# Engine order, edge layout and block exit changed together in a small message-passing kernel

## The chip, the cores and the metric

One core of a Trainium2 chip. The metric is the device time of one execution in microseconds. The kernel before takes 10.4 us, so this is a program of some 110 small instructions in which latencies and waits decide, not throughput.

The profile's span (first to last instruction) is shorter than the device time, 8.6 of 10.4 us before, and the difference stays out of the profile.

## The reference

128 nodes with 64 features, 512 edges with 32 features. Each edge makes a message from its source node and its own features, and each destination node takes the mean of its messages:

```python
src, dst = edge_index[0], edge_index[1]
for i in range(len(src)):
    msg_input = np.concatenate([node_features[src[i]], edge_features[i]])
    msg = np.maximum(0, msg_input @ W_msg)
    messages[dst[i]] += msg
    counts[dst[i]] += 1
return node_features + messages / np.maximum(counts, 1)[:, None]
```

## The kernel before

Gather and scatter are matmuls with one-hot matrices. The 512 source indices are cast to bf16, broadcast over 128 partitions by a matmul with ones, and compared with the partition number: this gives `gt_bf` (node x edge; its two halves are gt A and gt B below). `nf^T gt` (the gather) puts the source nodes' features, transposed, into the upper 64 rows of `xt_bf`; the edge features, transposed by TensorE, go into the lower 32. `xt_bf^T W` is the messages, a relu makes `m_bf`. A second one-hot, `d_bf` (edge x destination), sums messages and counts. Edges come in four chunks of 128; half A is chunks 0 and 1 (VectorE), half B chunks 2 and 3 (ScalarE).

The parts that the change touches, cut:

```python
# ScalarE
act.dma_start(ef_sb, edge_features.rearrange("(c p) f -> p c f", p=128))
act.dma_start(dcol_sb, bass.AP(ei_handle, n_edges, [[1, 128], [128, n_chunks]]))
wait(act, s_ef);   act.copy(ef_bf, ef_sb)
wait(act, s_xnTB); act.copy(xt_bf[0:node_dim, nhalf:n_edges], xnTB_ps)
wait(act, s_mB);   act.activation(m_bf[:, 2:4, :], mB_ps, Relu)
# VectorE, after the two casts of the source indices and the two halves of gt_bf
wait(dve, s_tp);   dve.tensor_copy(xt_bf[node_dim:feat_dim, :], efT_ps)   # transposed features
wait(dve, s_xnTA); dve.tensor_copy(xt_bf[0:node_dim, 0:nhalf], xnTA_ps)   # half A
wait(dve, s_dcf);  dve.tensor_tensor(d_bf[:, 0:2, :], ..., is_equal)      # one-hot A
dve.tensor_tensor(d_bf[:, 2:4, :], ..., is_equal)                         # one-hot B
wait(dve, s_mA);   dve.tensor_scalar(m_bf[:, 0:2, :], mA_ps, 0.0, max)    # relu A
...                                     # maximum of counts, reciprocal, result
# all engines
block = E(nc.Block(no_gpsimd_drain=True))
```

## Time and profile before

The median of 15 runs is 10.40 us (10.39 to 10.41). How to read the views: a timeline line is start, length (us), engine, source line, operation, output and inputs, shapes, and in brackets how long the engine sat idle and what ended that. The chain is followed back from the last instruction.

| Point in the profile before | us |
|---|---|
| source cast starts (index DMA has landed) | 2.26 |
| features' cast, start to end | 3.03 to 3.33 |
| transposes start | 3.38 |
| relu B ends (ScalarE) / relu A ends (VectorE) | 5.65 / 5.75 |
| result (last VectorE instruction) starts | 6.36 |
| span / device time | 8.6 / 10.40 |

The lines behind it are in the prediction below. "Front" means the part up to the transposes.

### The profile page before, as it was taken

Reading aid. Unit: us, or ns where it says so; the run is one execution under the profiler, and the core shown is the slowest. Engines: PE = TensorE matmul, PEld = TensorE weight load, DVE = VectorE, ACT = ScalarE, POOL = GpSimd, SP = SyncE. Lnnn points to the kernel's source line nnn. Section 1 sums busy time; section 2 is a strip of 40 time slices with the busy share of each in tenths; the row PEclk is TensorE's granted clock in tenths of the full one; section 3 lists DMA queues with packets and bytes.
Section 4 is the critical chain, followed back from the end, with each engine's and each line's share of the span. In section 5 each row is a group of like instructions: output and inputs, shape, how many; then the busy total and the mean of one; then the engine's idle time right before and its main releaser. Section 6 shows DMA issues by size and latency. Waiting matters only on the chain.

```text
span 8.6 us, 112 instructions
## 1 busy us (share of the span) xinstructions
PE 2.8 (32%) x20; PEld 1.4 (16%) x20; DVE 4.4 (51%) x17; ACT 2.2 (26%) x4; POOL 1.1 (13%) x9
## 2 busy tenths in 40 slices
PE   0000000000009983999991097099800000000000
PEld 0000000000004403928000090089000000000000
DVE  0001658910597099994989999975858000000000
ACT  0000000099999994000006900920000000000000
POOL 0801930000000090195000000000000000000000
DMA  0000000029969300000000000000000000060000
GB/s 0 0 0 0 0 0 0 19 43 146 197 77 62 60 7 0 0 0 0 0 0 0 0 0 0 0 0 0 0 0 0 0 0 0 1 148 4 0 0 0
DMA packets 1458, 0.16 MB, mean 19 GB/s; under 512 B 1457, under 2 KB 1457, under 8 KB 1458
## 3 DMA queue, kind: packets, MB, share of 16 engines
q10 hardware_dynamic: 1056, 0.07, 8.2%
q1 hardware_dynamic: 402, 0.09, 5.1%
HBM read 0.13 MB, written 0.03 MB: 19 GB/s over the span
## 4 chain that ended last, share of the span: by engine, by line
DVE 24%; ACT 18%; ACTq 11%; PE 10%; issue 5%; DVEq 0%
ACT L179 15%; PE efT_ps L220 7%; ACTq L171 6%; DVE xt_bf L346 5%; ACTq L162 5%; DVE xt_bf L344 5%; DVE d_bf L358 4%; DVE d_bf L349 4%; ACT ef_bf L179 4%; DVE res_sb L383 3%; PE cnt_ps L269 3%; DVE rcnt_sb L380 2%; DVE cnt_sb L378 2%; DVEq L42 0%
## 5 line engine op out<-in xcount | busy, mean ns | idle before, releaser
L179 ACT ACT_TABLE_LOAD x1 | 1.3, 1283 | 1.7 <-PEq L412 1.7
L198 PE MATMUL bankA_ps<-src_bf,ones_bf 1*128 1x256 bf16 x1 | 0.4, 388 | 2.6 <-DVE src_bf L316 2.6
L182 ACT CAST xt_bf<-bankB_ps 64x256 bf16<-64x256 f32 x1 | 0.4, 366 | 1.3 <-PE bankB_ps L236 1.3
L220 PE MATMUL efT_ps<-ident_bf,ef_bf 128*32 128x128 bf16 x4 | 0.6, 307 | 0.2 <-ACT ef_bf L179 0.2
L331 DVE TENSOR_SCALAR gt_bf<-bankA_ps,pidx_f 128x256 bf16<-128x256 f32 x1 | 0.5, 483 | 0.3 <-PE bankA_ps L198 0.3
L301 DVE MEMSET ones_bf<- 1x128 bf16 x1 | 0.2, 165 | 0.8 <-PEq L412 0.8
L316 DVE CAST src_bf<-ei_row 1x256 bf16<-1x256 int32 x1 | 0.3, 282 | 0.5 <-DMA ei_row<-in_edge_index_dram 0.5
L198 PEld LDWEIGHTS bankA_ps<-src_bf,ones_bf 1*128 1x128 bf16 x1 | 0.1, 98 | 2.6 <-DVE src_bf L316 2.6
L133 POOL CAST nf_bf<-nf_sb 128x64 bf16<-128x64 f32 x1 | 0.2, 236 | 1.9 <-DMA nf_sb<-in_node_features_dram 1.9
L344 DVE COPY xt_bf<-efT_ps 32x512 bf16<-32x512 bf16 x1 | 0.4, 415 | 0.1
L338 DVE TENSOR_SCALAR gt_bf<-bankB_ps,pidx_f 128x256 bf16<-128x256 f32 x1 | 0.5, 475 | 0.0
L346 DVE CAST xt_bf<-bankA_ps 64x256 bf16<-64x256 f32 x1 | 0.4, 417 | 0.0
L229 PE MATMUL bankA_ps<-gt_bf,nf_bf 128*64 128x256 bf16 x1 | 0.4, 423 | 0.0
L236 PE MATMUL bankB_ps<-gt_bf,nf_bf 128*64 128x256 bf16 x1 | 0.4, 421 | 0.0
L220 PEld LDWEIGHTS efT_ps<-ident_bf,ef_bf 128*32 128x32 bf16 x4 | 0.3, 127 | 0.5 <-ACT ef_bf L179 0.5
L247 PE MATMUL mA_ps<-w_bf,xt_bf 96*128 96x64 bf16 x2 | 0.3, 238 | 0.4 <-DVE xt_bf L346 0.4
L358 DVE TENSOR_TENSOR d_bf<-iota_bf,dcol_f 128x256 bf16<-128x256 bf16 x1 | 0.4, 410 | 0.0
L349 DVE TENSOR_TENSOR d_bf<-iota_bf,dcol_f 128x256 bf16<-128x256 bf16 x1 | 0.4, 409 | 0.0
L209 PE MATMUL bankB_ps<-src_bf,ones_bf 1*128 1x256 bf16 x1 | 0.4, 402 | 0.0
L186 ACT ACTIVATE m_bf<-mB_ps 128x128 bf16<-128x128 f32 x1 | 0.3, 277 | 0.4 <-PE mB_ps L258 0.4
L269 PE MATMUL cnt_ps<-onescol_bf,d_bf 128*128 128x1 bf16 x4 | 0.3, 170 | 0.3 <-DVE d_bf L358 0.3
L383 DVE SCALAR_TENSOR_TENSOR res_sb<-agg_ps,rcnt_sb,nf_sb 128x64 f32<-128x64 f32 x1 | 0.3, 283 | 0.1
(28 smaller groups left out, 5.1 us busy)
## 6 DMA issues: line engine op xcount, KB each, us to landing
ef_sb<-in_edge_features_dram ACTq DMA_DIRECT2D x1, 64.0 KB, 2.0
nf_sb<-in_node_features_dram SPq DMA_DIRECT2D x1, 32.0 KB, 1.8
out_dram<-res_sb SPq DMA_DIRECT2D x1, 32.0 KB, 1.5
w_sb<-in_W_msg_dram SPq DMA_DIRECT2D x1, 24.0 KB, 1.9
ei_row<-in_edge_index_dram SPq DMA_DIRECT2D x1, 4.0 KB
dcol_sb<-in_edge_index_dram ACTq DMA_DIRECT2D x1, 4.0 KB, 2.4
```

The source lines that it names most:

```text
L171: act.dma_start(dcol_sb[:, :], bass.AP(ei_handle, n_edges, [[1, 128], [128, n_chunks]]),),
L179: done(act.copy(ef_bf[:, :, :], ef_sb[:, :, :]), s_efbf)
L198: pe.matmul(bcastA_ps, ones_bf[:, :], src_bf[:, 0:nhalf], start=True, stop=True,),
L220: mm = pe.transpose(efT_ps[:, c * ncol : (c + 1) * ncol], ef_bf[:, c, :], ident_bf[:, :],)
L269: mm = pe.matmul(cnt_ps[:, :], d_bf[:, c, :], onescol_bf[:, :], start=(c == 0), stop=(c == n_chunks - 1),)
L331: dve.tensor_scalar(gt_bf[:, 0:nhalf], bcastA_ps, pidx_f[:, 0:1], None, ALU.is_equal),
L338: dve.tensor_scalar(gt_bf[:, nhalf:n_edges], bcastB_ps, pidx_f[:, 0:1], None, ALU.is_equal),
L344: done(dve.tensor_copy(xt_bf[node_dim:feat_dim, :], efT_ps[:, :]), s_xtef)
L346: done(dve.tensor_copy(xt_bf[0:node_dim, 0:nhalf], xnTA_ps), s_xcA)
L349: dve.tensor_tensor(d_bf[:, 0:2, :], bass.AP(iota_bf, 0, [[128, 128], [0, 2], [1, 128]]), bass.AP(dcol_f, 0, [[n_chunks, 128], [1, 2], [0, ...
L358: dve.tensor_tensor(d_bf[:, 2:4, :], bass.AP(iota_bf, 0, [[128, 128], [0, 2], [1, 128]]), bass.AP(dcol_f, 2, [[n_chunks, 128], [1, 2], [0, ...
L383: dve.scalar_tensor_tensor(res_sb[:, :], agg_ps[:, :], rcnt_sb[:, 0:1], nf_sb[:, :], ALU.mult, ALU.add,),
```

## The change

The intent: fewer and larger pieces per DMA, a shorter front on ScalarE, and less queueing on VectorE. Its core, cut (renamings `nhalf` to `wa` and `2` to `n_a`, and PSUM tensors that become separate, are left out):

```diff
-            edge_features.rearrange("(c p) f -> p c f", p=128)      # ScalarE: 512 pieces of 128 B
+            edge_features.rearrange("(p c) f -> p c f", c=n_chunks) # 128 pieces of 512 B
-            act.dma_start(dcol_sb, AP(ei_handle, n_edges, [[1, 128], [128, n_chunks]]))
+            sync.dma_start(dcol_sb, AP(ei_handle, n_edges, [[n_chunks, 128], [1, n_chunks]]))
+            wait(act, s_tp)
+            act.copy(xt_bf[node_dim:feat_dim, :], efT_ps)           # from VectorE
-            two casts src_bf[:, 0:nhalf], src_bf[:, nhalf:n_edges]
+            one cast src_bf[:, :]
-                    src_bf[:, 0:nhalf],                             # broadcast matmul, read dense
+                    bass.AP(src_bf, 0, [[n_edges, 1], [1, n_a], [n_chunks, ncol]]),
 VectorE:
-            transposed features; half A; one-hot A; one-hot B; relu A
+            one-hot A; half A; one-hot B; relu A
 TensorE:
-            wait(pe, s_dB); four count matmuls
+            wait(pe, s_dA); two count matmuls; wait(pe, s_dB); two count matmuls
-        block = E(nc.Block(no_gpsimd_drain=True))
+        block = E(nc.Block())
```

More of the change, by code (lines that the diff above doesn't have):

```diff
@@ L27, in bass_mpnn_update_kernel @@
     ncol = n_edges // n_chunks
-    nhalf = n_edges // 2
+    n_a = 2
+    wa = n_a * ncol
+    wb = n_edges - wa
     ei_handle = edge_index.tensor
@@ L68, in bass_mpnn_update_kernel @@
         rcnt_sb = E(nc.sbuf_tensor("rcnt_sb", [128, 1], fp32))
+        act_dummy = E(nc.sbuf_tensor("act_dummy", [128, 1], fp32))
         res_sb = E(nc.sbuf_tensor("res_sb", [n_nodes, node_dim], fp32))
-        bankA_ps = E(nc.psum_tensor("bankA_ps", [128, n_edges], fp32))
-        bankB_ps = E(nc.psum_tensor("bankB_ps", [128, n_edges], fp32))
+        bcastA_t = E(nc.psum_tensor("bcastA_ps", [128, wa], fp32))
+        xnTA_t = E(nc.psum_tensor("xnTA_ps", [node_dim, wa], fp32))
+        bankB_ps = E(nc.psum_tensor("bankB_ps", [128, 2 * wb], fp32))
         efT_ps = E(nc.psum_tensor("efT_ps", [edge_dim, n_edges], bf16))
-        mA_ps = E(nc.psum_tensor("mA_ps", [128, 2 * node_dim], fp32))
-        mB_ps = E(nc.psum_tensor("mB_ps", [128, 2 * node_dim], fp32))
+        mA_ps = E(nc.psum_tensor("mA_ps", [128, n_a * node_dim], fp32))
+        mB_ps = E(nc.psum_tensor("mB_ps", [128, (n_chunks - n_a) * node_dim], fp32))
         cnt_ps = E(nc.psum_tensor("cnt_ps", [n_nodes, 1], fp32))
         agg_ps = E(nc.psum_tensor("agg_ps", [n_nodes, node_dim], fp32))
-        bcastA_ps = bankA_ps[:, 0:nhalf]
-        bcastB_ps = bankB_ps[:, 0:nhalf]
-        xnTA_ps = bankA_ps[0:node_dim, nhalf:n_edges]
-        xnTB_ps = bankB_ps[0:node_dim, nhalf:n_edges]
+        bcastA_ps = bcastA_t[:, :]
+        xnTA_ps = xnTA_t[:, :]
+        bcastB_ps = bankB_ps[:, 0:wb]
+        xnTB_ps = bankB_ps[0:node_dim, wb : 2 * wb]
         s_ei = _Sig("s_ei", 16)
@@ L92, in bass_mpnn_update_kernel @@
         s_efbf = _Sig("s_efbf")
-        s_sqA = _Sig("s_sqA")
-        s_sqB = _Sig("s_sqB")
+        s_sq = _Sig("s_sq")
         s_bcA = _Sig("s_bcA")
@@ L156, in _ @@
             done(sync.dma_start(nf_sb[:, :], node_features), s_nf, 16)
+            done(
+                sync.dma_start(
+                    dcol_sb[:, :],
+                    bass.AP(ei_handle, n_edges, [[n_chunks, 128], [1, n_chunks]]),
+                ),
+                s_dc,
+                16,
+            )
             done(sync.dma_start(w_sb[:, :], W_msg), s_w, 16)
@@ L163, in _ @@
                     ef_sb[:, :, :],
-                    edge_features.rearrange("(c p) f -> p c f", p=128),
+                    edge_features.rearrange("(p c) f -> p c f", c=n_chunks),
                 ),
@@ L168, in _ @@
             )
-            with nc.allow_non_contiguous_dma(reason="dst column gather"):
-                done(
-                    act.dma_start(
-                        dcol_sb[:, :],
-                        bass.AP(ei_handle, n_edges, [[1, 128], [128, n_chunks]]),
-                    ),
-                    s_dc,
-                    16,
-                )
             wait(act, s_ef)
             done(act.copy(ef_bf[:, :, :], ef_sb[:, :, :]), s_efbf)
+            wait(act, s_tp)
+            done(act.copy(xt_bf[node_dim:feat_dim, :], efT_ps[:, :]), s_xtef)
             wait(act, s_xnTB)
-            done(
-                act.copy(xt_bf[0:node_dim, nhalf:n_edges], xnTB_ps), s_xcB
-            )
+            done(act.copy(xt_bf[0:node_dim, wa:n_edges], xnTB_ps), s_xcB)
             wait(act, s_mB)
@@ L186, in _ @@
                 act.activation(
-                    m_bf[:, 2:4, :],
-                    mB_ps[:, :].rearrange("p (c d) -> p c d", c=2),
+                    m_bf[:, n_a:n_chunks, :],
+                    mB_ps[:, :].rearrange("p (c d) -> p c d", c=n_chunks - n_a),
                     ACTF.Relu,
@@ L195, in _ @@
         def _(pe):
-            wait(pe, s_sqA, s_cst)
+            wait(pe, s_sq, s_cst)
             done(
@@ L206, in _ @@
             )
-            wait(pe, s_sqB)
             done(
@@ L211, in _ @@
                     ones_bf[:, :],
-                    src_bf[:, nhalf:n_edges],
+                    bass.AP(src_bf, n_a, [[n_edges, 1], [1, n_chunks - n_a], [n_chunks, ncol]]),
                     start=True,
@@ L228, in _ @@
             done(
-                pe.matmul(
-                    xnTA_ps, nf_bf[:, :], gt_bf[:, 0:nhalf], start=True, stop=True
-                ),
+                pe.matmul(xnTA_ps, nf_bf[:, :], gt_bf[:, 0:wa], start=True, stop=True),
                 s_xnTA,
@@ L236, in _ @@
                 pe.matmul(
-                    xnTB_ps,
-                    nf_bf[:, :],
-                    gt_bf[:, nhalf:n_edges],
-                    start=True,
-                    stop=True,
+                    xnTB_ps, nf_bf[:, :], gt_bf[:, wa:n_edges], start=True, stop=True
                 ),
@@ L245, in _ @@
             wait(pe, s_xcA, s_xtef, s_wbf)
-            for c in range(2):
+            for c in range(n_a):
                 mm = pe.matmul(
@@ L253, in _ @@
                 )
-                if c == 1:
+                if c == n_a - 1:
                     done(mm, s_mA)
             wait(pe, s_xcB)
-            for c in range(2, 4):
+            for c in range(n_a, n_chunks):
                 mm = pe.matmul(
-                    mB_ps[:, (c - 2) * node_dim : (c - 1) * node_dim],
+                    mB_ps[:, (c - n_a) * node_dim : (c - n_a + 1) * node_dim],
                     xt_bf[:, c * ncol : (c + 1) * ncol],
@@ L264, in _ @@
                 )
-                if c == 3:
+                if c == n_chunks - 1:
                     done(mm, s_mB)
+            wait(pe, s_dA)
+            for c in range(n_a):
+                pe.matmul(
+                    cnt_ps[:, :],
+                    d_bf[:, c, :],
+                    onescol_bf[:, :],
+                    start=(c == 0),
+                    stop=False,
+                )
             wait(pe, s_dB)
-            for c in range(n_chunks):
+            for c in range(n_a, n_chunks):
                 mm = pe.matmul(
@@ L272, in _ @@
                     onescol_bf[:, :],
-                    start=(c == 0),
+                    start=False,
                     stop=(c == n_chunks - 1),
@@ L277, in _ @@
                     done(mm, s_cntps)
-            wait(pe, s_reluA, s_dA)
-            for c in range(2):
+            wait(pe, s_reluA)
+            for c in range(n_a):
                 pe.matmul(
@@ L287, in _ @@
             wait(pe, s_reluB)
-            for c in range(2, 4):
+            for c in range(n_a, n_chunks):
                 mm = pe.matmul(
@@ L293, in _ @@
                     start=False,
-                    stop=(c == 3),
+                    stop=(c == n_chunks - 1),
                 )
-                if c == 3:
+                if c == n_chunks - 1:
                     done(mm, s_agg)
@@ L316, in _ @@
                 dve.tensor_copy(
-                    src_bf[:, 0:nhalf],
-                    bass.AP(eir32.tensor, 0, [[2 * n_edges, 1], [2, nhalf]]),
-                ),
-                s_sqA,
-            )
-            done(
-                dve.tensor_copy(
-                    src_bf[:, nhalf:n_edges],
-                    bass.AP(eir32.tensor, 2 * nhalf, [[2 * n_edges, 1], [2, nhalf]]),
-                ),
-                s_sqB,
+                    src_bf[:, :],
+                    bass.AP(eir32.tensor, 0, [[2 * n_edges, 1], [2, n_edges]]),
+                ),
+                s_sq,
             )
@@ L331, in _ @@
                 dve.tensor_scalar(
-                    gt_bf[:, 0:nhalf], bcastA_ps, pidx_f[:, 0:1], None, ALU.is_equal
+                    gt_bf[:, 0:wa], bcastA_ps, pidx_f[:, 0:1], None, ALU.is_equal
                 ),
@@ L338, in _ @@
                 dve.tensor_scalar(
-                    gt_bf[:, nhalf:n_edges], bcastB_ps, pidx_f[:, 0:1], None, ALU.is_equal
+                    gt_bf[:, wa:n_edges], bcastB_ps, pidx_f[:, 0:1], None, ALU.is_equal
                 ),
@@ L342, in _ @@
             )
-            wait(dve, s_tp)
-            done(dve.tensor_copy(xt_bf[node_dim:feat_dim, :], efT_ps[:, :]), s_xtef)
-            wait(dve, s_xnTA)
-            done(dve.tensor_copy(xt_bf[0:node_dim, 0:nhalf], xnTA_ps), s_xcA)
             wait(dve, s_dcf, s_ibf)
@@ L349, in _ @@
                 dve.tensor_tensor(
-                    d_bf[:, 0:2, :],
-                    bass.AP(iota_bf, 0, [[128, 128], [0, 2], [1, 128]]),
-                    bass.AP(dcol_f, 0, [[n_chunks, 128], [1, 2], [0, 128]]),
+                    d_bf[:, 0:n_a, :],
+                    bass.AP(iota_bf, 0, [[128, 128], [0, n_a], [1, 128]]),
+                    bass.AP(dcol_f, 0, [[n_chunks, 128], [1, n_a], [0, 128]]),
                     ALU.is_equal,
@@ L356, in _ @@
             )
+            wait(dve, s_xnTA)
+            done(dve.tensor_copy(xt_bf[0:node_dim, 0:wa], xnTA_ps), s_xcA)
             done(
                 dve.tensor_tensor(
-                    d_bf[:, 2:4, :],
-                    bass.AP(iota_bf, 0, [[128, 128], [0, 2], [1, 128]]),
-                    bass.AP(dcol_f, 2, [[n_chunks, 128], [1, 2], [0, 128]]),
+                    d_bf[:, n_a:n_chunks, :],
+                    bass.AP(iota_bf, 0, [[128, 128], [0, n_chunks - n_a], [1, 128]]),
+                    bass.AP(dcol_f, n_a, [[n_chunks, 128], [1, n_chunks - n_a], [0, 128]]),
                     ALU.is_equal,
@@ L368, in _ @@
                 dve.tensor_scalar(
-                    m_bf[:, 0:2, :],
-                    mA_ps[:, :].rearrange("p (c d) -> p c d", c=2),
+                    m_bf[:, 0:n_a, :],
+                    mA_ps[:, :].rearrange("p (c d) -> p c d", c=n_a),
                     0.0,
```

## The prediction

> **What bounds the kernel now.** I read four views: the page's rows by line, the DMA issues, the chain that ended last, and the timeline. The chain comes first, because a 10.4 us program of 112 small instructions is a matter of latencies, not of busy shares (no engine is above 51% of the span). Columns: start us, length us, what.
>
> ```profile
> 0.74 0.40 ACTq L162
> ...
> 1.17 0.53 ACTq L171
> ...
> 1.73 1.28 ACT L179
> ...
> 3.03 0.31 ACT ef_bf L179
> ...
> 3.38 0.62 PE efT_ps L220 x4
> ...
> 4.02 0.39 DVE xt_bf L344
> ...
> 4.47 0.42 DVE xt_bf L346
> 4.88 0.33 DVE d_bf L349
> 5.22 0.34 DVE d_bf L358
> ...
> 5.61 0.28 PE cnt_ps L269 x4
> ```
>
> The end is set by the edge features. ScalarE issues two DMAs, loads its table, casts the features; TensorE transposes them; VectorE copies the transpose out, then works through a queue of its own (node half A, two builds of the one-hot d_bf); after the last build come the counts, their reciprocal and the result at 6.36 us. There is a second chain beside it, from the source indices. It is on no page of the critical chain, but the timeline has it (start us, length us, engine, line, tile):
>
> ```profile
> 2.26 0.28 DVE L316 CAST src_bf<-ei_row 1x256 bf16<-1x256 int32 x1 [0.50 <-DMA ei_row<-in_edge_index_dram]
> 2.60 0.39 PE L198 MATMUL bankA_ps<-src_bf,ones_bf 1*128 1x256 bf16 x1 [2.60 <-DVE src_bf L316]
> 3.02 0.48 DVE L331 TENSOR_SCALAR gt_bf<-bankA_ps,pidx_f 128x256 bf16<-128x256 f32 x1 [0.28 <-PE bankA_ps L198]
> 3.42 0.47 DVE L338 TENSOR_SCALAR gt_bf<-bankB_ps,pidx_f 128x256 bf16<-128x256 f32 x1
> 4.13 0.42 PE L236 MATMUL bankB_ps<-gt_bf,nf_bf 128*64 128x256 bf16 x1
> 4.58 0.37 ACT L182 CAST xt_bf<-bankB_ps 64x256 bf16<-64x256 f32 x1 [1.26 <-PE bankB_ps L236]
> 5.37 0.28 ACT L186 ACTIVATE m_bf<-mB_ps 128x128 bf16<-128x128 f32 x1 [0.42 <-PE mB_ps L258]
> 5.47 0.28 DVE L368 TENSOR_SCALAR m_bf<-mA_ps 128x128 bf16<-128x128 f32 x1
> 5.81 0.29 PE L280 MATMUL agg_ps<-m_bf,d_bf 128*128 128x64 bf16 x2
> ```
>
> Half B of the messages is ready at 5.37 + 0.28 = 5.65 us on ScalarE. The aggregation does not start until 5.81, because half A's relu on VectorE, though its matmul (first start 4.94) was long done, sat behind the two d_bf builds and ended at 5.75; the counts are later still. So VectorE's queue between 4.0 and 5.75 us is the bound of the tail, and the front of the chain (ScalarE's DMA issues and table load) delays when that queue begins.
>
> **What the Trainium skill says.** (1) "ScalarE: Activation LUTs", section What ACT_TABLE_LOAD costs: about 1283 ns for a load. The trace has 1283 ns, and it begins at 1.73 us, right behind the second DMA issue (1.17 + 0.53 = 1.70) and not behind the features. (2) Same page and section: an ACTIVATE with immediate scale and bias takes 186 ns + 0.833 N ns. For N = 256 that is 399 ns; the trace has 366 (L182), for N = 128 from PSUM 277 (L186) against 293. It is a few per cent high here. (3) "SBUF — State Buffer", the note on 16-byte cachelines in the port section: at least two hits per line are needed for full bandwidth. No strided bf16 read by TensorE is in this trace, so it cannot agree or disagree. (4) "DMA: Bandwidth & Descriptors", the summary table: 512 B or more per descriptor for line rate. The page of before has 1457 of 1458 packets under 512 B; the two ScalarE DMAs, whose patterns make 512 pieces each, took 2.0 and 2.4 us to landing, the 32 KB node features 1.8.
>
> **The change part by part.**
>
> *The DMA layout.* Edge p·4+c instead of c·128+p: the features become 128 pieces of 512 B instead of 512 of 128 B, the destinations 128 pieces of 32 B instead of 512 of 8 B. The destination DMA moves to SyncE between node features and weights. ScalarE loses 0.53 us of issue, so its table load starts at about 1.17 to 1.20 and ends near 2.48. The features I take to land at 2.5 (estimate: 0.74 + 1.8, the node features' landing, for 2.0). The cast is then 2.5 to 2.85 instead of 3.03 to 3.33. That is up to 0.5 us off the front of the old chain. On SyncE the third issue at 1.51 is now the destinations; with 1.8 to 1.9 to landing they arrive at about 3.4 (3.57 before), cast by GpSimd by 3.6. The weights slip by one issue, 0.4 us, from 1.51 to 1.9; landing 1.9 later is 3.8, cast done by about 4.1; needed at 4.75. Neither binds.
>
> *One source cast instead of two.* A 128x1 cast takes 155 ns (L304), a 1x256 one 282 ns: 127 ns for 255 elements, 0.5 ns each (128x128 at 218 ns gives the same slope). So 1x512 takes 155 + 511 x 0.5 = 410 ns. It replaces a first half that was ready after 282, so the start of the index chain is 0.13 us later. This is a loss.
>
> *The transpose copy moves from VectorE to ScalarE.* Off VectorE: 0.415 us (L344) and its wait for the transposes. On ScalarE: by the slope of 277 to 366 ns per 128 elements, 366 + 2 x 89 = 544 ns; by the skill's formula 613. Transposes now run about 3.1 to 3.7, so the copy ends at 4.3 to 4.35, before ScalarE's next work (4.5). Hidden.
>
> *Order on VectorE.* The first d_bf build goes into the hole before node half A, the second after it; the relu of half A then meets no queue. Counts are split, so two of four matmuls run early.
>
> *The index chain, which should now set the end*, with lengths and gaps from the rows above. Source cast 2.26 + 0.41 = 2.67; gap 0.06 (2.54 to 2.60), broadcast A 2.73; 0.42 from matmul to VectorE, gt A 3.15, ending 3.63; 0.40 from start to start, gt B 3.55, ending 4.02; gap 0.05, gather matmul B 4.07; 0.45 to ScalarE, copy B 4.52 to 4.89; gap 0.05, message matmuls B 4.94; 0.33 (5.04 to 5.37), relu B 5.27 to 5.55; gap 0.06, aggregation B 5.61; 0.30 for both matmuls and 0.05 to VectorE, result 5.96.
>
> *VectorE beside it.* d_bf A 3.95 (0.40 after gt B), half A copy 4.28 (0.33 later) to 4.70, d_bf B 4.62 to 5.03. Message matmuls A 4.75, relu A 4.75 + 0.33 = 5.08 to 5.36. Counts 5.08; 0.30 to their maximum 5.38; 0.20 to the reciprocal 5.58; 0.25 to the result 5.83. That is 0.13 earlier than 5.96, so aggregation B decides.
>
> The result then starts at 5.96 instead of 6.36: minus 0.40 us. The output DMA and the end are unchanged. The 1.8 us between the 8.6 us span and the 10.4 us time I take as constant. 10.40 - 0.40 = 10.00; I add 0.02 for the block's exit (below).
>
> *PSUM split, unused act_dummy.* No instruction, no time. In before, no reader of bankA overlaps a writer (gt A ends 3.50, its next matmul starts 3.91).
>
> *The default block exit.* It drops the option that leaves out a GpSimd drain. No page that I found gives its length, and before has none. GpSimd's last cast ends at 3.98 (about 4.1 after the change) and the output lands at 6.67 + 1.5 = 8.17, so 4 us of drain would be hidden if it runs before the engines meet.
>
> **The rivals.** (a) *The drain costs at the end.* If it, or a heavier barrier, stands after the output's landing, its length adds in full: from 0.2 us (gain down to 0.2, time 10.2) to more than 0.4 (no gain). For: before spends 0.4 us after landing on the exit, so what the exit does is visible. Against: GpSimd is idle for half of the kernel. (b) *The strided read of src_bf is slow.* Two bf16 values 8 B apart share a 16-byte line, just the two hits that the skill asks. If it failed and the matmul streamed at half speed, 0.1 to 0.2 us would come on the index chain: 10.1 to 10.2. (c) *The index DMA lands earlier.* It is one 4 KB packet and shares engines with the features' 512 packets; with 128 of them it may land sooner and everything follows: 9.8 to 9.9. Against: the DMA row shows 19 GB/s in the slice from 1.5 to 1.72 us, which is 4 KB, just its size, before the bulk. (d) *The moved load waits.* If the destinations landed after 3.8 us, the first d_bf build, now ahead of half A in VectorE's order, would hold that half: 0.1 to 0.3 us worse.
>
> **Range and chances.** Centre 10.02. (c) or a shorter cast gives 9.8; (a) or (b) at moderate size 10.3. Faster by 2% means below 10.19: it takes the loss of more than 0.17 of 0.38 to miss. I give 0.74 to that, 0.20 to within 2%, and 0.06 to slower, which nearly only a costly exit could bring.
>
> **What would show it.** Right: table load at about 1.2; features' cast ending before 2.9; a source cast of about 410 ns; gt A near 3.15; no VectorE queue ahead of relu A; result near 5.96; the chain running from the index DMA over half B and the relu on ScalarE. Wrong: broadcast to gt A over 0.5 us (b); d_bf A waiting for the destinations (d); a span longer by more than the result's shift (a); a result that starts on time and a time that does not follow (the exit outside the span).

## The result, and the profile after

The median of 11 runs is 9.88 us (9.82 to 10.02), against 10.40 for before in the same session. The ratio is 0.948 (95% interval 0.9455 to 0.9504). Ratios here are the mean time of one kernel's fast runs over that of the other's of the same rounds, so they are not quite the ratio of the quoted medians. A run is labelled slow here when it is over 1.5% above the fastest run of its kernel; three of these eleven are (10.00 to 10.02).

The chain of the kernel after (start us, length us, what):

```profile
0.74 1.40 DMA ei_row<-in_edge_index_dram
...
2.16 0.43 DVE src_bf L320
...
2.64 0.41 PE bcastA_ps L200
...
3.47 0.47 DVE gt_bf L335
3.94 0.33 DVE d_bf L342
4.27 0.34 DVE xt_bf L351
...
4.66 0.30 PE mA_ps L242 x2
...
4.98 0.30 DVE m_bf L363
...
5.33 0.29 PE agg_ps L284 x2
5.62 0.22 PE agg_ps L293 x2
...
5.86 0.28 DVE res_sb L378
```

It begins with another DMA: not the features but the source indices. The table load, 15% of the chain before, is gone from it. After gt B it runs over half A on VectorE. That half will turn out not to be the one that decides. What lies beside it, from the timeline of after:

```profile
1.13 1.28 ACT L181 ACT_TABLE_LOAD   x1 [1.13 <-PEq L407]
...
2.53 0.30 ACT L181 CAST ef_bf<-ef_sb 128x128 bf16<-128x128 f32 x1
...
3.18 0.61 PE L221 MATMUL efT_ps<-ident_bf,ef_bf 128*32 128x128 bf16 x4
...
3.82 0.57 ACT L183 COPY xt_bf<-efT_ps 32x512 bf16<-32x512 bf16 x1 [0.99 <-PE efT_ps L221]
...
3.90 0.47 POOL L147 CAST w_bf<-w_sb 96x64 bf16<-96x64 f32 x1 [0.50 <-DMA w_sb<-in_W_msg_dram]
...
4.00 0.42 PE L235 MATMUL bankB_ps<-gt_bf,nf_bf 128*64 128x256 bf16 x1
...
5.20 0.28 ACT L188 ACTIVATE m_bf<-mB_ps 128x128 bf16<-128x128 f32 x1 [0.38 <-PE mB_ps L253]
...
5.53 0.29 PE L293 MATMUL agg_ps<-m_bf,d_bf 128*128 128x64 bf16 x2
```

The features are ready at 2.83 us, 0.50 earlier than before, but the transposes start at 3.18, only 0.20 earlier: TensorE takes its work in program order, and the broadcast matmuls, now the later ones (2.64 and 2.85), stand ahead. In eight more profiles whose features were ready earlier the transposes follow the second broadcast by the same 0.33 or 0.34 us. Relu B ends at 5.48 and half B's aggregation starts at 5.53, right behind it.

A table of three intervals sorts the difference of the two profiled runs, and serves for every experiment:

| Profiled run | A: source cast starts | B: cast to result | C: result to end of device time | Time |
|---|---|---|---|---|
| before | 2.26 | 4.10 | 4.04 | 10.40 |
| after | 2.16 | 3.70 | 3.97 | 9.83 |
| difference | -0.10 | -0.40 | -0.07 | -0.57 |

B is the work between the landing of the indices and the result. C is the profiled run's time minus the start of the result, so it holds the result, the output's DMA, the exit and what lies outside the span. The table sorts the difference; it doesn't yet say what caused it, since in before the front, and not the landing of the indices, sets when the result starts.

### The profile page after: what moved, and what is told of

It reads as the page before. It is cut to its first block, busy times and chain, and to the rows that moved or that the text cites. A ratio compares the mean times of both kernels' runs of the same rounds, so it can differ in the third digit from the quotient of the medians.

```text
span 8.0 us, 107 instructions
## 1 busy us (share of the span) xinstructions
PE 2.9 (36%) x20; PEld 1.4 (18%) x20; DVE 3.9 (49%) x15; ACT 2.8 (35%) x5; POOL 1.4 (18%) x9
## 4 chain that ended last, share of the span: by engine, by line
DVE 30%; DMA 17%; PE 15%; issue 6%
DMA ei_row<-in_edge_index_dram 17%; DVE gt_bf L335 6%; DVE src_bf L320 5%; PE bcastA_ps L200 5%; DVE xt_bf L351 4%; DVE d_bf L342 4%; PE mA_ps L242 4%; DVE m_bf L363 4%; PE agg_ps L284 4%; DVE res_sb L378 4%; DVE gt_bf L328 3%; PE agg_ps L293 3%
## 5 line engine op out<-in xcount | busy, mean ns | idle before, releaser
L183 ACT COPY xt_bf<-efT_ps 32x512 bf16<-32x512 bf16 x1 | 0.6, 572 | 1.0 <-PE efT_ps L221 1.0
L328 DVE TENSOR_SCALAR gt_bf<-bcastA_ps,pidx_f 128x256 bf16<-128x256 f32 x1 | 0.5, 484 | 0.5 <-PE bcastA_ps L200 0.5
L147 POOL CAST w_bf<-w_sb 96x64 bf16<-96x64 f32 x1 | 0.5, 465 | 0.5 <-DMA w_sb<-in_W_msg_dram 0.5
```

Of the source, the lines that this page charges most:

```text
L147: done(pool.tensor_copy(w_bf[:, :], w_sb[:, :]), s_wbf)
L183: done(act.copy(xt_bf[node_dim:feat_dim, :], efT_ps[:, :]), s_xtef)
L328: dve.tensor_scalar(gt_bf[:, 0:wa], bcastA_ps, pidx_f[:, 0:1], None, ALU.is_equal),
```

## The experiments

The theory to test: the engine order gives the 0.40 us of B; the layout's gain at the front lies off the path; the new end is set by the index chain through half B. The rivals: the layout, or the exit, is what pays; half A sets the end, as the profile's chain has it.

Each experiment is after with the edit shown, if not said otherwise.

### One part at a time: exit, layout, order

**after_no_drain** and **before_drain** swap the exits of the two kernels.

```diff
 after_no_drain:
-        block = E(nc.Block())
+        block = E(nc.Block(no_gpsimd_drain=True))
 before_drain (from before):
-        block = E(nc.Block(no_gpsimd_drain=True))
+        block = E(nc.Block())
```

> The kernel after with the block exit of before (GpSimd drain left out again). My account: the exit's drain is hidden behind 4 us of idle GpSimd, so the time stays at 9.88 us within 0.05, ratio 0.945 to 0.953. Rival (a), the default exit costs something after the output's landing: the time falls by what it costs, to 9.7 or less, and the tail from the result to the end of the span shrinks.

> The kernel before with the default block exit of after, the same question from the other side, on a kernel whose runs scatter by only 0.02 us. My account: 10.40 within 0.03. Rival (a): 10.5 or more.

Before with the default exit takes 10.34 us (10.31 to 10.36) against 10.40, ratio 0.9935 (0.9919 to 0.9951). The profiles have the result at 6.36 us in both, so nothing moved ahead of it; C falls from 4.04 to 3.96, and the page counts 109 instructions instead of 112. After without it: 10.02 us (9.91 to 10.19), three of six runs with the slow label; the fast ones give 0.9533 (0.9519 to 0.9548) instead of 0.948, and C is 4.05. In all twelve profiles with the default exit C is 3.95 to 3.99, in the two without it 4.04 and 4.05. The drain is not merely hidden, as I had it; the exit that has it is shorter by 0.06 to 0.08 us on both kernels. That is the opposite of my allowance and of rival (a). Which of its instructions saves the time, the profile doesn't show.

The profiled run of after_no_drain was one of its slow ones, at 10.12 us:

```profile
2.37 0.41 DVE L320 CAST src_bf<-ei_row 1x512 bf16<-1x512 int32 x1 [0.61 <-DMA ei_row<-in_edge_index_dram]
...
6.07 0.28 DVE L378 SCALAR_TENSOR_TENSOR res_sb<-agg_ps,rcnt_sb,nf_sb 128x64 f32<-128x64 f32 x1 [0.22 <-PE agg_ps L293]
```

B is again 3.70 us (6.07 - 2.37). All of the delay lies in A: the indices landed 1.61 us after their issue instead of 1.40. The clock is the same. So what is labelled slow here is the late landing of one DMA. The other profiled run with that label (two_casts, cast at 2.35) shows it too, and so do two of runs labelled fast (features_later and delay_a).

**layout_only** keeps the layout, the queues, the merged cast and the exit, and gives VectorE and ScalarE back their old order; the counts wait for both one-hots.

```diff
 ScalarE:
-            wait(act, s_tp)
-            act.copy(xt_bf[node_dim:feat_dim, :], efT_ps)
 VectorE:
-            one-hot A; half A; one-hot B
+            wait(dve, s_tp)
+            dve.tensor_copy(xt_bf[node_dim:feat_dim, :], efT_ps)
+            half A; one-hot A; one-hot B
```

> The change's data layout alone: features and destinations contiguous per partition, destinations on SyncE's queue, one source cast, but VectorE's old order (transpose copy on VectorE, half A, then both one-hot builds). My account, stepped through with the durations of after: one-hot B ends 5.40, counts 5.45, result 6.20 instead of 6.36, so about 10.2 us (0.16 off). Rival, the layout is the main part because it takes 0.5 us off the old front: 9.95 or less.

10.51 us (10.33 to 10.58), ratio of fast runs 0.9974 (0.9936 to 1.0013): no gain. Four of the six runs carry the slow label. The profiled run is the fastest, 10.33 us:

```profile
3.95 0.42 DVE L339 COPY xt_bf<-efT_ps 32x512 bf16<-32x512 bf16 x1
...
5.63 0.19 PE L262 MATMUL cnt_ps<-onescol_bf,d_bf 128*128 128x1 bf16 x2 [0.36 <-DVE d_bf L353]
...
6.36 0.28 DVE L378 SCALAR_TENSOR_TENSOR res_sb<-agg_ps,rcnt_sb,nf_sb 128x64 f32<-128x64 f32 x1
```

Its result starts at 6.36, just where it does in before, and the 0.07 us are the exit's (C is 3.97). My 6.20 was too early in two places: half A follows the 512-column copy on VectorE by 0.45 us, as it does in before, where I had 0.38; and this variant's counts start at 5.63, 0.15 after one-hot B instead of 0.06. The second isn't the layout's doing but, it seems, the variant's, in which TensorE waits there for both one-hots; so the layout with the old order may be worth up to 0.09 us. The rival, that the layout is the main part, falls all the same. The features' cast ends 0.42 us earlier than in before (2.91), but VectorE's old queue starts only 0.07 earlier (3.95 for 4.02): it now stands behind gt B, so behind the index chain. The PSUM split is in this run too; with the old order it brings no gain either.

**order_only** keeps the order and the exit, and takes layout, queues and the two source casts from before.

```diff
-            edge_features.rearrange("(p c) f -> p c f", c=n_chunks)
+            edge_features.rearrange("(c p) f -> p c f", p=128)
-            sync.dma_start(dcol_sb, AP(ei_handle, n_edges, [[n_chunks, 128], [1, n_chunks]]))
+            act.dma_start(dcol_sb, AP(ei_handle, n_edges, [[1, 128], [128, n_chunks]]))
-            one cast of 512; broadcast matmuls read with a stride of 4
+            two casts of 256; broadcast matmuls read densely
```

> The change's engine order alone: transpose copy on ScalarE, one-hot A ahead of half A, counts split; layout, queues and the two source casts as in before. My account: transposes at 3.38, gather B still at 4.13 behind them, copy B 4.58, relu B 5.33 to 5.61, aggregation B 5.67, result about 6.02, so about 10.06 us (0.34 off, two thirds of the 0.52). And since the front is then set by the table load and not by a DMA's landing, its runs should scatter as little as those of before (0.02 us), not as those of after (0.2 us). Rival, order alone is worth little because the front still delays everything: 10.25 or more.

10.00 us, all five runs within 10.00 to 10.02, ratio 0.9622 (0.9608 to 0.9635). The result starts at 6.02, as expected to the hundredth (0.34 us off); the time is lower than my 10.06 by the exit's 0.06. The chain still has the old front:

```profile
1.73 1.28 ACT L183
...
3.37 0.61 PE efT_ps L224 x4
3.98 0.37 PE xnTA_ps L233
```

and, from its timeline, the result:

```profile
6.02 0.28 DVE L388 SCALAR_TENSOR_TENSOR res_sb<-agg_ps,rcnt_sb,nf_sb 128x64 f32<-128x64 f32 x1 [0.21 <-PE agg_ps L296]
```

The table load sets the front, and the scatter is gone, as expected. That the index DMA has room there, so that its landing no longer shows, is one reading. The other is that it lands steadily beside the old layout's DMAs: the three profiles with that layout have the source cast at 2.25 to 2.29. No run decides between them. Nor does a run separate the three edits of the order (the copy on ScalarE, one-hot A ahead of half A, the split counts); the 0.34 us belong to all three together.

### Which half sets the end

**delay_b** and **delay_a** put one useless copy ahead of one relu each.

```diff
 delay_b (ScalarE):
             wait(act, s_mB)
+            act.copy(act_dummy[:, :], pidx_f[:, :])
 delay_a (VectorE):
             wait(dve, s_mA)
+            dve.tensor_copy(act_dummy[:, :], pidx_f[:, :])
```

> After, with one useless ScalarE copy of 128x1 between the wait for half B's messages and its relu. Which half sets the end? My account is half B (relu B ends 5.48, aggregation B starts 5.53): source cast to result grows from 3.70 us by the whole length added ahead of relu B, 0.09 to 0.19. Rival, the profile's own chain, which runs over half A's relu on VectorE and both aggregations: it grows by less than 0.05.

> The counterpart of delay_b: after, with one useless VectorE copy of 128x1 between the wait for half A's messages and its relu. delay_b moved relu B by 0.10 us and the result by 0.09 (source cast to result 3.79 instead of 3.70). My account, half B sets the end and half A has about 0.10 us of room (its first aggregation matmul at 5.33, the second pair not before 5.53): a delay of 0.07 leaves source cast to result at 3.70 to 3.72. Rival, both halves are in step, as the profile's chain over half A suggests: 3.77 or more.

delay_b, from its timeline:

```profile
2.14 0.42 DVE L321 CAST src_bf<-ei_row 1x512 bf16<-1x512 int32 x1 [0.38 <-DMA ei_row<-in_edge_index_dram]
...
5.27 0.27 ACT L189 ACTIVATE m_bf<-mB_ps 128x128 bf16<-128x128 f32 x1
...
5.93 0.28 DVE L379 SCALAR_TENSOR_TENSOR res_sb<-agg_ps,rcnt_sb,nf_sb 128x64 f32<-128x64 f32 x1 [0.31 <-PE agg_ps L294]
```

delay_a:

```profile
2.35 0.41 DVE L320 CAST src_bf<-ei_row 1x512 bf16<-1x512 int32 x1 [0.60 <-DMA ei_row<-in_edge_index_dram]
...
5.58 0.29 PE L284 MATMUL agg_ps<-m_bf,d_bf 128*128 128x64 bf16 x2
...
6.05 0.28 DVE L379 SCALAR_TENSOR_TENSOR res_sb<-agg_ps,rcnt_sb,nf_sb 128x64 f32<-128x64 f32 x1 [0.22 <-PE agg_ps L293]
```

Relu B starts 3.13 us after the source cast instead of 3.04 (5.20 - 2.16), and B grows by the same 0.09, to 3.79. Half A's aggregation starts 3.23 after it instead of 3.17, and B stays at 3.70. Half B sets the end, shown from both sides, and half A has at least 0.06 us of room. The profile's chain names half A because, at TensorE, it steps from half B's aggregation to the instruction before it. Times (two runs each: delay_b 9.88 and 9.91, delay_a 9.93 and 10.02) would have said the reverse, since delay_a's profile caught a late landing, 2.35.

### The merged source cast

**two_casts** makes two casts again, which bring the edges into the new order as they read; the broadcast matmuls then read densely.

```diff
-                    bass.AP(eir32.tensor, 0, [[2 * n_edges, 1], [2, n_edges]])           # 512
+                    bass.AP(eir32.tensor, 0, [[2 * n_edges, 1], [2, n_a], [2 * n_chunks, ncol]])
+                    ... and the same from 2 * n_a for half B
```

> After, with the merged source cast undone: two casts of 256 that also put the edges in order while they read (their reads stride 32 B), so the matmul reads densely. My account, that the merge was the one losing part of the change: first cast 282 ns instead of 416, everything behind it 0.13 us earlier, source cast to result 3.57 us instead of 3.70, time about 9.75 at the fast end. Rival: the strided cast reads cost as much as the merge did, or the transposes (3.18 to 3.79 in after) now hold the gather matmul, and source cast to result stays at 3.65 to 3.70.

10.06 us (9.84 to 10.11), five of six runs with the slow label, no ratio. The profile has B at 3.70 (6.05 - 2.35): nothing gained. Both parts of the rival show:

```profile
2.35 0.38 DVE L322 CAST src_bf<-ei_row 1x256 bf16<-1x256 int32 x1 [0.59 <-DMA ei_row<-in_edge_index_dram]
...
3.41 0.61 PE L223 MATMUL efT_ps<-ident_bf,ef_bf 128*32 128x128 bf16 x4
```

A cast of 256 with reads 32 B apart takes 376 ns, not 282, and the second cast (to 3.03) puts broadcast B at 3.08 and the transposes at 3.41, behind which gather A starts at 3.95, though gt A ended at 3.69. On half B, which sets the end, gather B starts 1.81 us after the cast (4.16) instead of 1.84, and its copy stands at 4.65 behind ScalarE's copy of the transposes (4.05 to 4.62): 2.30 us after the cast, as in after (4.46 - 2.16).

**half_layout** tries to have both: edge h*256 + 2p + c, so that half A is the first 256 indices in memory.

```diff
-            edge_features.rearrange("(p c) f -> p c f", c=n_chunks)
+            edge_features.rearrange("(h p c) f -> p h c f", h=2, c=n_a)      # 256 pieces of 256 B
-            bass.AP(ei_handle, n_edges, [[n_chunks, 128], [1, n_chunks]])
+            bass.AP(ei_handle, n_edges, [[n_a, 128], [wa, 2], [1, n_a]])     # 256 pieces of 16 B
-            one cast of 512; broadcast matmuls read with a stride of 4
+            two dense casts of 256; broadcast matmuls read with a stride of 2
```

> After, with a layout between the two: edge h*256 + 2p + c, so half A is the first 256 source indices, the cast is two dense casts of 256 again (282 ns each), features in 256 pieces of 256 B, destinations in 256 pieces of 16 B. My account, that the merged cast cost 0.13 us on the chain that sets the end: source cast to result 3.57 to 3.60 us instead of 3.70, and against the control 0.10 to 0.13 us less. Rival: the smaller pieces land the indices later (1.50 to 1.55 us as in before), or the transposes again hold the gather matmul, and the time is that of the control or more.

9.88 us (9.80 to 9.97), ratio 0.9472 (0.9424 to 0.952). Its control, **after_again**, is after unchanged, in the same rounds:

> The kernel after, unchanged, as a control beside the next two on the same chip: 9.82 to 10.02 us as before, with its scatter. The profile's source cast to result should again be 3.70 us, whatever the time; if the scatter is all in the index DMA's landing, time minus the start of the source cast is the same (9.83 - 2.16 = 7.67 us) within 0.03 in this profile too.

10.02 us (9.86 to 10.12), ratio 0.9613 (0.9558 to 0.9669). So half_layout is the fastest kernel of these rounds. Its profile has the casts at 282 and 274 ns, and B at 3.70 all the same:

```profile
2.22 0.28 DVE L322 CAST src_bf<-ei_row 1x256 bf16<-1x256 int32 x1 [0.46 <-DMA ei_row<-in_edge_index_dram]
...
3.92 0.42 PE L237 MATMUL bankB_ps<-gt_bf,nf_bf 128*64 128x256 bf16 x1
...
4.83 0.27 PE L244 MATMUL mA_ps<-w_bf,xt_bf 96*128 96x64 bf16 x2 [0.49 <-POOL w_bf L148]
```

Up to gather B the gain is there: 1.70 us after the cast (3.92 - 2.22) instead of 1.84 (4.00 - 2.16), 0.14 us. Then it is lost: the weights land 2.2 us after issue instead of 1.8, their cast on GpSimd ends at 4.69, and the messages, ready otherwise, wait for it until 4.83; those of half B start at 4.91, 2.69 us after the cast instead of 2.72. On half A the transposes hold gather A for 0.24 us (gt A ended at 3.47, gather A starts at 3.71), but they hold it in after as well, for 0.16 (3.55 to 3.71). So the merged cast cost about what the sum said, and a late weight load took the place of it in this profile. Whether its absence is why half_layout is faster isn't shown: the landings differ from run to run, and six runs of each are no proof of a better kernel. The control's own profile has B at 3.73, because the node features landed late (2.3 us after issue), and C at 3.96.

### The index DMA and the scatter

After runs from 9.82 to 10.02 us in its first session and from 9.86 to 10.12 in the control; order_only scatters by 0.02, and before by 0.02 to 0.05, but for one run of 10.54 in the control's rounds. Three experiments went for the index DMA.

**features_later**: ScalarE waits for VectorE's constants before the features' DMA.

```diff
         def _(act):
+            wait(act, s_cst)
```

> After, with ScalarE waiting for VectorE's two constants (about 1.0 us) before it issues the features' DMA. Two readings of the scatter of after (9.82 to 10.02): the features' packets of 512 B get into the way of the one 4 KB packet of the source indices in some executions. If so, the indices land at 1.40 us after issue in every run, the scatter falls to 0.05 us or less with all runs near 9.85, and the later features cost nothing, since the transposes start at 3.18 behind the broadcast matmuls anyway while the features' cast ended at 2.83. Rival: the scatter is the index DMA's own; then the runs still spread by 0.2 us.

9.99 us (9.91 to 10.06). The features were issued at 1.04 instead of 0.73, and the profiled run still had the indices at 2.33. So the features' packets are not the cause, or not alone. That later features cost nothing holds in this run (B is 3.70), which had the late landing. Their cast ends at 3.24, after the 3.18 at which after with the early landing starts its transposes, so for that case it isn't shown.

**index_alone**: besides, the node features wait until 1.5 us, and the destinations go behind the features on ScalarE.

```diff
+            wait(act, s_cst)                # ahead of the features
+            wait(sync, s_ibf)               # ahead of the node features
-            sync.dma_start(dcol_sb, ...)
+            act.dma_start(dcol_sb, ...)
```

> After, with the index DMA alone at first: features wait for VectorE's constants (about 1.0 us), the node features for VectorE's iota copy (about 1.47 us, on the index DMA's own queue), the destinations go behind the features on ScalarE. If other transfers' packets cause the late landings (1.6 us instead of 1.4), all runs are now near the early landing and scatter by 0.05 us or less, near 9.85 to 9.9. Rival: the landing is scattered by itself, and the runs still spread over 0.15 us or more.

10.20 to 10.21 us in four runs. No scatter, but not for the reason in question, and the experiment is badly made: the destinations' issue on ScalarE pushed the table load to 1.92, the features' cast to 3.21 and gather B to 4.32, behind the transposes. B is 3.98, and the front sets the end as it did in before. It doesn't tell why the indices land late. Against features_later, the table load is 0.45 us later (1.92 for 1.47) and the result 0.18 (6.21 for 6.03), although the indices landed 0.10 earlier.

**index_in_16**: the 4 KB of indices in pieces of 256 B, into a row with gaps.

```diff
-                    ei_row[:, :],
-                    bass.AP(ei_handle, 0, [[n_edges, 1], [1, n_edges]]),
+                    bass.AP(ei_row, 0, [[16 * 33, 1], [33, 16], [1, 32]]),
+                    bass.AP(ei_handle, 0, [[n_edges, 1], [32, 16], [1, 32]]),
```

> After, with the source indices' 4 KB loaded as 16 pieces of 256 B into a row with gaps (so that they stay apart), read by one cast. Account: one packet of 4 KB on one DMA engine is what lands at 1.40 or 1.61 us; in 16 pieces it lands earlier by the transfer time of the large packet[...] and the time goes to 9.7 to 9.8. Rival: more pieces meet the features' packets on more engines, the last of them decides, and the landing stays at 1.4 to 1.6 or grows; or the cast of 16 short runs is slower than 416 ns.

10.46 us (10.39 to 10.54), a clear miss. Issuing took 0.59 us instead of 0.34, landing 2.0, and the source cast started at 2.80. B is again 3.70, and time minus the start of the cast is 7.67 (10.47 - 2.80), as in after (9.83 - 2.16): what the landing loses, the time loses to the hundredth.

So why one and the same 4 KB transfer lands after 1.40 us in one execution and 1.6 in another stays open.

## Why the prediction was right, point by point

The time, 9.88, lies in the range, and faster was the likeliest outcome. The mechanism was right, not only the number. Step by step:

- **The index chain through half B sets the end.** Right, shown by delay_b and delay_a. The predicted length from source cast to result, 5.96 - 2.26 = 3.70 us, is what the trace shows, and the steps between hold within 0.04 us (gather B 1.81 predicted, 1.84 measured; copy B 2.26 and 2.30; aggregation B 3.35 and 3.37). The sign it named, a chain over half B in the profile, did not appear; it took the delays to show it.
- **The order on VectorE and the copy on ScalarE.** Right, and the main part: 0.34 us in order_only, for both and the split counts together. The copy took 572 ns, between the two estimates, 544 by the slope and 613 by the skill's formula, and lay hidden. (The prediction calls the formula a few per cent high. By its own numbers it is 9% at 256 columns and 6% at 128.)
- **The DMA layout takes up to 0.5 us off the front.** Right in size (2.83 for 3.33) and in that it is off the path: layout_only gains nothing, though its own late counts may hide up to 0.09 us. What the full change has over order_only (10.00) is -0.12 us by the first session's median and +0.02 by the control's; I can't call it a gain.
- **The merged cast.** Its length was right (416 ns for 410). That it is a loss of 0.13 us shows in half_layout as far as gather B (0.14). No run shows that undoing it brings the result forward: two_casts and half_layout leave B at 3.70, each through other waits.
- **The exit.** The sign was wrong: +0.02 predicted, -0.06 to -0.08 measured, on both kernels.
- **Rival (b), slow strided reads by TensorE.** Did not occur: 0.43 us from the start of the broadcast matmul to gt A for 0.42.
- **Rival (c), an earlier index DMA.** Occurred by half, in some executions: of the profiles with the 512 B pieces and the single index packet, four have the source cast at 2.14 to 2.17, one at 2.23, four at 2.33 to 2.37. My argument against it, the 4 KB ahead of the bulk, did not settle it. I had not foreseen that, once the table load is off the path, this DMA's scatter becomes the kernel's.
- **Rival (d), a late destination load.** Did not occur: its cast is done at 3.40, one-hot A starts at 3.86 right behind gt B.

The distance of the profiled run from the middle, 9.83 for 10.02, is the landing (0.10) and the exit (0.02 allowed, 0.07 gained). The first it had as rival (c), the second with the wrong sign. Two profiled variants with B at 3.70 do take the predicted middle (features_later 10.01, delay_a 10.02), but by luck: there a landing later than before's covers the gained exit.

## What to carry to other kernels

Look for the first engine queue in which finished work waits behind unrelated work: here one VectorE queue held back the end, and 0.4 us gained at the features ahead of it were worth at most 0.1, because the queue also had to wait for the indices. When an experiment's times scatter, split the time at the landing of the data that starts the chain; the interval behind it repeated within 0.03 us in the profiles of after, its control and after_no_drain, where the whole varied by 0.29. And test which of two parallel branches decides by delaying each one; the profile's chain can follow the wrong one.

## What the Trainium skill lacked or had wrong

- "DMA: Bandwidth & Descriptors", Latency and other measured facts: no figure for the scatter of one small load. Here the same 4 KB index load took 1.40 to 1.63 us from issue to its first use, in nine profiles (2.14 to 2.37 us minus 0.74).
- The same page, Why a DMA increments its semaphore by 16 and not by 1, tells how a transfer spreads over engines, not that it can cost: 4 KB into one partition cut into pieces of 256 B was issued in 0.59 us for 0.34, and its cast started at 2.80 us instead of the 2.14 to 2.37 of nine profiles with one piece.
- No page that I found has the cost of the block's exit: the default was 0.06 to 0.08 us shorter than the one that leaves out GpSimd's drain.
- "SBUF — State Buffer", the note on 16-byte cachelines, agrees with what is measured here, but neither it nor another page that I found has a figure for a one-source cast on VectorE with spaced reads: one of 256 int32 elements took 282 ns with reads 8 B apart (two in a line) and 376 ns with reads 32 B apart. For TensorE, reading bf16 8 B apart cost no more than 0.01 us (0.43 us from matmul to gt A for 0.42).
- "SBUF — State Buffer", Summary: rules for kernel authors, says that where a VectorE instruction has two SBUF inputs and the GpSimd one reads SBUF, the second to issue fully blocks until the first finishes. The traces agree that the second one loses, but not by the whole overlap (spans on GpSimd are rough in the profile): the weights' cast on GpSimd, begun 0.04 us into one-hot A (3.86 to 4.27), took 465 ns instead of 232, which ends it at 4.37, not at 4.50; in after_again, where it began first, at 3.83, it took its 233 ns and one-hot A, begun at 3.87, 483 instead of 414.
- "ScalarE: Activation LUTs", What ACT_TABLE_LOAD costs: an estimate by its 186 ns + 0.833 N gives 613 ns for the 512-column copy from PSUM; the trace has 572.
